# The U buffers of b, f and g moved by 64 bytes, and two pairs of buffers exchanged

## The chip, the cores and the metric

The kernel runs on one core of one Trainium2 chip. A core has five engines with queues of their own: TensorE (PE, matmuls; its weight loads are shown apart as PEld), VectorE (DVE), ScalarE (ACT), GpSimd (POOL) and SyncE (SP, which only issues transfers). They work on SBUF, 128 partitions of on-chip memory; TensorE writes its sums to PSUM, eight banks of 2 KB a partition. The metric is the time of one execution on the device in microseconds (us), as a median of several.

## The reference

One layer of a streaming encoder, on 1024 positions of 1024 channels in float32:

```python
u = rms_norm(x, pre_norm)
z, bg, cg, v = jnp.split(u @ w_in, 4, axis=-1)          # w_in: 1024 x 8192
y = bg * causal_dwconv(cg * v, conv_w) * jax.nn.silu(z)  # three taps, 2048 channels
out = x + rms_norm(y @ w_out, post_norm)                 # w_out: 2048 x 1024
```

Nearly all arithmetic is in the two matrix products, 1024 x 1024 x 8192 and 1024 x 2048 x 1024.

## The kernel before

**Two halves of a number.** A float32 value is split into a high part, rounded to the type that TensorE multiplies (`F32R`, four bytes), and a low part, the rest (`split`: ScalarE copies, VectorE subtracts). One product of two such operands takes three matmuls: low weights by high data, high weights by low data, high weights by high data (`product`, L810). Each of the 4320 matmuls has a weight load of its own, of 128 columns.

**Seven products for eight.** The input product is cut into 2 x 2 blocks, and seven products of sums and differences of blocks, named a to g, take the place of eight. The normed and transposed input, in the seven combinations that the products need, stays in SBUF as seven **U buffers**, u_a to u_g. Each is a tile of 16,384 bytes a partition, `[128, 2, 4, 512]`: a high and a low half, each of four blocks of 128 rows by 512 positions. The weights pass by in 32 *pairs* of column blocks (two pairs, p = 2c and 2c + 1, make one of 16 *chunks*, c), each split into a `wh` and a `wl` tile. So a **wide** product (a, c, d or e of a pair) is twelve matmuls that stream 512 positions of a U buffer past weights that lie in *pages*.

**Once more for b, f and g.** From chunk 2 on, the products b, f and g (f up to chunk 14, g up to chunk 13) are themselves cut in 2 x 2 and done by seven smaller products, a' to g' (`deep_product`, L1404). Such a **narrow** product is six matmuls of 256 positions. Four of the seven, a', b', e' and f', stream a quarter of the U buffer; c', d' and g' stream combinations that lie in tiles of their own, called `ub` (`ubch_deep`, `ufdl_deep` and so on, 2,048 bytes each, in the pool `tmp` behind `gpad`).

**The output product** uses the same scheme. The U buffers are free by then, and their space is taken, buffer by buffer, by the split operands: `ou_` (w_out, the moving operand) and `oy_` (the result y, the weights) for the halves 0 and 1 of a, c, e, d and g (`split_pages`, L1552, and `third_unit`, L1536, for `ou_a1`), and `oA`, `oB` and `ox` for the small products of b and f (`split_small`). Here the moving operand and the weights both lie in U buffers.

**Where things lie.** SBUF is filled in the order of the pools: 1,024 bytes for DMA descriptors, `const`, `small`, `up` (seven buffers of 16,384 bytes from address 3136), `pages` (32 pages of 2,048 bytes from 117824), and then `head` or `tmp` or `p2` in turn from 183360. All addresses here are bytes within a partition. Modulo 128 the U buffers and the pages lie at 64, the ub tiles at 96. The names in the trace are those of the tiles: `px<-u_d,wdh` is a matmul that sums into the PSUM bank px, streams u_d and has weights from wdh; `px2b`, `pv2f` and the like are banks of narrow products, `po_`, `pb_`, `pf_` those of the output product.

**The order of the work.** The program records all operations, and a planner (`Plan.arrange`) puts them in an order for each engine by modelled costs and due times, then emits them (`Plan.emit`, L604). It counts U buffers as one pool of seven and does not know where a buffer lies. Which of the seven an allocation gets is decided on emission: in the kernel before by the pool, in the order in which buffers come free. Because every engine operation passes through one helper, the profile gives the same line, L252, for all of them; so tiles tell them apart.

Of the kernel before, what the change touches and what calls it, by code (L numbers as in the profile page):

```python
# [11 lines left out]
F32 = mybir.dt.float32  # L12
# [77 lines left out]
class View:  # L90
# [3 lines left out]
    def __init__(self, tile, steps, ids, dtype):  # L94
        self.tile, self.steps, self.ids, self.dtype = tile, steps, ids, dtype
# [88 lines left out]
class Pool:  # L184
# [4 lines left out]
    def tile(self, shape, dtype, **kw):  # L189
        t = Tile(self, list(shape), dtype, kw)  # L190
        self.plan.room.setdefault(t.key, kw.get("bufs", self.bufs))
        if not self.plan.recording:
            if kw["tag"] == "pg":
                t.slot = self.plan.slots.pop(0)
            t.get()
            self.plan.taken.setdefault(t.key, []).append(t)
        return t


class Op:  # L200

    __slots__ = ("lock", "order", "base", "move", "others", "lead", "est", "engine", "name", "args", "kw", "n", "needs", "feeds", "dur", "lat", "waits", "late", "tiles", "news", "start", "ideal", "pos", "soft")


class Engine:
# [409 lines left out]
def kernel(  # L615
# [35 lines left out]

    const = plan.pool(ctx.enter_context(tc.tile_pool(name="const", bufs=1)), 1)
    small = plan.pool(ctx.enter_context(tc.tile_pool(name="small", bufs=2)), 2)
    up = plan.pool(ctx.enter_context(tc.tile_pool(name="up", bufs=7)), 7)
    pages = plan.pool(ctx.enter_context(tc.tile_pool(name="pages", bufs=PAGES)), PAGES)
    psum = plan.pool(ctx.enter_context(tc.tile_pool(name="psum", bufs=8, space=bass.MemoryType.PSUM)), 8, "psum")
    dram = plan.pool(ctx.enter_context(tc.tile_pool(name="dram", bufs=1, space=bass.MemoryType.DRAM)), 1, "dram")
# [962 lines left out]
    slots = [("a", 2), ("b", 2)]  # L1620
# [445 lines left out]
```

## Time and profile before

| | us |
|---|---|
| median of 3 runs (772.88 to 773.8) | 773.35 |
| the profiled execution | 772.83 |
| its span, first to last instruction | 771.0 |
| TensorE busy | 762.2 |
| VectorE busy | 673.9 |
| ScalarE busy | 458.8 |
| GpSimd busy | 462.2 |

The granted clock of TensorE was 0.998 of full speed. In the profile "x12" is a count of instructions; a shape such as `128*128 128x256` gives the weights (rows * columns) and the result. The start of a matmul is recorded, its end is modelled, and a matmul's duration overlaps the start of the next. So the time that one takes from the path is the distance between starts.

### The profile page before, as it was taken

Reading aid. Unit: us, or ns where it says so; the run is one execution under the profiler, and the core shown is the slowest. Engines: PE = TensorE matmul, PEld = TensorE weight load, DVE = VectorE, ACT = ScalarE, POOL = GpSimd, SP = SyncE. Lnnn points to the kernel's source line nnn. Section 1 sums busy time; section 2 is a strip of 40 time slices with the busy share of each in tenths; the row PEclk is TensorE's granted clock in tenths of the full one; section 3 lists DMA queues with packets and bytes.
Section 4 is the critical chain, followed back from the end, with each engine's and each line's share of the span. In section 5 each row is a group of like instructions: output and inputs, shape, how many; then the busy total and the mean of one; then the engine's idle time right before and its main releaser. Section 6 shows DMA issues by size and latency. Waiting matters only on the chain.

```text
span 771.0 us, 12816 instructions
## 1 busy us (share of the span) xinstructions
PE 762.2 (99%) x4320; PEld 669.6 (87%) x4320; DVE 673.9 (87%) x1022; ACT 458.8 (60%) x880; POOL 462.2 (60%) x416
## 2 busy tenths in 40 slices
PE   8999999999999999999999999999999999999996
PEld 7888889898889898888888898988888889889885
DVE  6899988989988978989999989798999898877993
ACT  7765678575656565556556565556653656564831
POOL 2519997889575778696789777584739100600321
PEclk9999999999999999999999999999999999999999
DMA  9222325243333547576858474927465998666842
GB/s 318 66 56 82 119 85 152 101 126 131 97 116 96 171 111 209 126 191 158 239 137 254 116 215 107 249 84 213 122 180 174 335 367 293 197 218 206 274 150 109
DMA packets 117137, 130.11 MB, mean 169 GB/s; under 512 B 7320, under 2 KB 74704, under 8 KB 116944
## 3 DMA queue, kind: packets, MB, share of 16 engines
q1 hardware_dynamic: 112560, 120.77, 49.0%
q0 software_dynamic: 4352, 8.39, 7.1%
q8 instruction: 34, 0.56, 0.3%
q14 instruction: 31, 0.25, 0.1%
q10 hardware_dynamic: 160, 0.14, 0.0%
HBM read 101.74 MB, written 44.30 MB: 189 GB/s over the span
## 4 chain that ended last, share of the span: by engine, by line
PE 98%; DVE 1%; DMA 0%; ACT 0%; POOL 0%; issue 0%; POOLq 0%; ACTq 0%
PE px L252 39%; PE pv L252 15%; PE po_x L252 11%; PE px2b L252 5%; PE px2f L252 4%; PE px2g L252 3%; PE po_v L252 3%; PE pp L252 3%; PE pv2b L252 3%; PE pv2f L252 2%; PE pf_x L252 1%; PE pb_x L252 1%; PE py2b L252 1%; PE pv2g L252 1%; PE py L252 1%; PE pf_v L252 1%
## 5 line engine op out<-in xcount | busy, mean ns | idle before, releaser
L252 PE MATMUL px<-u_d,wdh 128*128 128x512 f32 x248 | 76.8, 390 | 0.0
L252 PE MATMUL px<-u_a,wah 128*128 128x512 f32 x248 | 76.7, 390 | 0.0
L252 PE MATMUL pv<-u_e,weh 128*128 128x512 f32 x248 | 76.7, 390 | 0.0
L252 PE MATMUL px<-u_c,wch 128*128 128x512 f32 x248 | 76.6, 390 | 0.0
L252 ACT COPY beside<-raw 128x512 f32<-128x512 f32 x67 | 39.6, 591 | 31.8 <-DVE wal L252 11.0
L252 PEld LDWEIGHTS px<-u_d,wdh 128*128 128x128 f32 x248 | 46.6, 188 | 9.1
L252 PEld LDWEIGHTS px<-u_c,wch 128*128 128x128 f32 x248 | 46.7, 188 | 9.0
L252 PEld LDWEIGHTS px<-u_a,wah 128*128 128x128 f32 x248 | 46.7, 188 | 8.9
L252 PEld LDWEIGHTS pv<-u_e,weh 128*128 128x128 f32 x248 | 46.6, 188 | 8.9
L252 DVE SCALAR_TENSOR_TENSOR cv<-gpad,cw,cv 128x1024 f32<-128x1024 f32 x32 | 49.7, 1554 | 3.4 <-ACT cv L252 3.3
L252 POOL TENSOR_TENSOR sf<-raw,sc 128x512 f32<-128x512 f32 x30 | 44.5, 1482 | 10.9 <-DVE sc L252 6.0
L252 PE MATMUL px<-u_d,wdl 128*128 128x512 f32 x124 | 48.7, 393 | 0.0
L252 PE MATMUL px<-u_a,wal 128*128 128x512 f32 x124 | 48.7, 393 | 0.0
L252 PE MATMUL px<-u_c,wcl 128*128 128x512 f32 x124 | 48.5, 392 | 0.0
L252 PE MATMUL pv<-u_e,wel 128*128 128x512 f32 x124 | 48.5, 391 | 0.0
L252 POOL TENSOR_TENSOR sc<-se,raw 128x512 f32<-128x512 f32 x25 | 36.5, 1460 | 19.0 <-DVE se L252 10.0
L252 ACT COPY sna<-px 128x512 f32<-128x512 f32 x30 | 17.6, 586 | 49.4 <-PE px L252 47.7
L252 POOL TENSOR_TENSOR raw<-raw,raw 128x512 f32<-128x512 f32 x31 | 44.8, 1446 | 3.3 <-DVE se L252 1.9
L252 POOL TENSOR_TENSOR rs_post<-ve_post,minus_half 128x1 f32<-128x1 f32 x7 | 5.4, 784 | 68.1 <-DVE ve_post L252 68.1
L252 POOL TENSOR_TENSOR se<-raw,raw 128x512 f32<-128x512 f32 x22 | 33.1, 1504 | 17.7 <-DMA raw<-in_sc_w_in 5.7
L252 DVE TENSOR_TENSOR wcl<-sc,wch 128x512 fp32r<-128x512 f32 x31 | 31.6, 1020 | 2.6 <-ACT wch L252 2.6
L252 DVE TENSOR_TENSOR sna<-px2b,sna 128x256 f32<-128x256 f32 x56 | 23.2, 413 | 11.9 <-PE px2b L252 11.9
(486 smaller groups left out, 2637.1 us busy)
## 6 DMA issues: line engine op xcount, KB each, us to landing
raw<-in_sc_w_in SPq DMA_DIRECT2D x128, 256.0 KB, 4.6
y_d<-cv SPq DMA_DIRECT2D x16, 512.0 KB, 3.1
s_d<-s SPq DMA_DIRECT2D x32, 256.0 KB, 4.8
t_d<-in_sc_w_out POOLq DMA_DIRECT2D x16, 512.0 KB, 8.2
tb<-in_sc_w_out SPq DMA_DIRECT2D x16, 256.0 KB, 3.0
t_d<-in_sc_w_out SPq DMA_DIRECT2D x16, 256.0 KB, 4.5
t_d<-t_d SPq DMA_DIRECT2D x16, 256.0 KB, 4.5
s<-y_d SPq DMA_DIRECT2D x16, 256.0 KB, 4.7
```

The lines of the kernel that those rows point to most:

```text
L252: getattr(engine, name)(*(self.plain(a) for a in args), **{k: self.plain(a) for k, a in kw.items()})
```

## The change

The pool of seven buffers is replaced by two pools with a gap behind each. Buffers 1, 2, 5 and 6 (those of d, c, a and e) keep their addresses modulo 128. Behind them come 64 unused bytes, then buffers 0, 3 and 4 (of g, f and b), then 448 unused bytes, so that pages and all that follows move by 512 bytes in all. Modulo 128 the U buffers of b, f and g then lie at 0, those of a, c, d and e, and the pages, still at 64, the ub tiles at 96.

A list says which buffer each allocation takes. It is the order that the pool chose before, but for two exchanges in the output stage: `ou_a1` takes buffer 4 and `oy_a1` buffer 6 (before: 6 and 4), and `oy_g0` takes buffer 6 and `ou_g0` buffer 3 (before: 3 and 6).

```diff
+U_LAYOUT = (
+    ((1,2,5,6,), 64),
+    ((0,3,4,), 448),
+)
+U_SLOTS = (5, 4, 2, 6, 1, 3, 0, 0, 5, 2, 4, 6, 1, 3, 0, 5, 2, 6, 4, 1, 6, 3, 0, 2, 4, 5, 6, 1, 0, 3, 2, 4, 5, 6, 0, 4, 1, 5, 6, 3, 2, 0)
+
+def gap(ctx, tc, name, size):
+    if size:
+        ctx.enter_context(tc.tile_pool(name=name, bufs=1)).tile([128, size // 4], F32, tag=name, name=name)
+
+class Shelves:
+    def __init__(self, ctx, tc):
+        self.at, self.slots = {}, list(U_SLOTS)
+        for n, (slots, room) in enumerate(U_LAYOUT):
+            pool = ctx.enter_context(tc.tile_pool(name=f"up{n}", bufs=1))
+            self.at.update({s: pool for s in slots})
+            gap(ctx, tc, f"room{n}", room)
+
+    def tile(self, shape, dtype, tag, **kw):
+        s = self.slots.pop(0)
+        return self.at[s].tile(shape, dtype, tag=f"u{s}", **dict(kw, bufs=1))
...
-    up = plan.pool(ctx.enter_context(tc.tile_pool(name="up", bufs=7)), 7)
+    up = plan.pool(Shelves(ctx, tc), 7)
```

The slots in the order of allocation are: u_a, u_b, u_c, u_e, u_d, u_f, the second half of x (`xb`), u_g; then ou_a0, oy_a0, ou_a1, oy_a1, oB1_b, oB3_b, oA1_b, oA2_b, oB2_b, oA3_b, ox_b, oy_c0, ou_c0, oy_c1, ou_c1, oy_e0, ou_e0, oy_e1, ou_e1, oA1_f, oB1_f, oB2_f, oA2_f, oA3_f, oB3_f, ox_f, ou_d0, oy_d0, oy_d1, ou_d1, oy_g0, ou_g0, oy_g1, ou_g1.

## The prediction

> **What bounds the kernel now.** I read the page first, from the top, for the engine that never rests; then the chain that ended last, inside two short windows, for the length of one product; then the timeline of TensorE, for the distance from one matmul's start to the next.
>
> ```profile
> span 771.0 us, 12816 instructions
> PE 762.2 (99%) x4320; PEld 669.6 (87%) x4320; DVE 673.9 (87%) x1022; ACT 458.8 (60%) x880; POOL 462.2 (60%) x416
> PEclk9999999999999999999999999999999999999999
> PE 98%; DVE 1%; DMA 0%; ACT 0%; POOL 0%; issue 0%; POOLq 0%; ACTq 0%
> ```
>
> TensorE is busy for 762.2 of 771.0 us at full clock, and 98% of the chain lies on it. Other engines are hardly waited for. The change adds and removes no instruction, so beside a wait at the exchanged buffers it can move the time in one way: through the spacing of the 4320 matmuls. A busy share cannot show a spacing, because neighbouring matmuls overlap. The chain, cut into products, can. First a piece before the narrow products begin, then pieces from the middle:
>
> ```profile
> 72.51 2.72 PE pv L252 x12
> ```
> ```profile
> 272.38 2.75 PE px L252 x12
> 275.13 0.70 PE px2b L252 x6
> 275.83 0.70 PE pv L252 x6
> 276.53 0.72 PE px L252 x6
> 277.25 0.72 PE px2g L252 x6
> ```
>
> The twelve-matmul pieces are wide products (512 columns); six-matmul pieces are narrow ones (256 columns). Equal narrow products differ: 0.70 us and 0.72 us. Their operands are seen in the timeline (first column start, second duration):
>
> ```profile
> 275.67 0.28 PE L252 MATMUL pv<-ufgh_deep,dwf 128*128 128x256 f32 x1
> ...
> 276.37 0.28 PE L252 MATMUL px<-u_g,dwg0l 128*128 128x256 f32 x1
> 276.49 0.40 PE L252 MATMUL px<-u_g,dwg0h 128*128 128x256 f32 x2
> 276.73 0.28 PE L252 MATMUL px<-u_g,dwg0l 128*128 128x256 f32 x1
> ...
> 277.81 0.40 PE L252 MATMUL px<-u_a,wal 128*128 128x512 f32 x1
> ...
> 279.20 0.39 PE L252 MATMUL px<-u_a,wal 128*128 128x512 f32 x1
> ...
> 280.56 0.28 PE L252 MATMUL px<-u_g,dwg2l 128*128 128x256 f32 x1
> 280.67 0.28 PE L252 MATMUL px<-u_g,dwg2h 128*128 128x256 f32 x1
> ```
>
> From 275.67 to 276.37 lie six matmuls that stream a ub tile: 0.70 / 6 = 116.7 ns each. From 276.37 to 277.81 lie twelve that stream u_g: 1.44 / 12 = 120.0 ns each. Both groups multiply 256 columns with weights from pages. What differs is the address of the moving operand against that of the weights. Counted through the pools, the U buffers begin at 3136 = 24*128 + 64, and the pages at 117824, also 64 past a multiple of 128. gpad has 4104 bytes, rounded up to a multiple of 32, so the ub tiles behind it begin 96 past one. Relative to the weights the U buffers lie at 0 and the ub tiles at +32 bytes (modulo 128), and +32 is 3.3 ns a matmul faster. The weight loads differ in the same way:
>
> ```profile
> L252 PEld LDWEIGHTS px2b<-ubgh_deep,dwb 128*128 128x128 f32 x56 | 9.5, 188 | 0.5
> L252 PEld LDWEIGHTS py2b<-u_b,dwb0h 128*128 128x128 f32 x56 | 8.7, 192 | 0.0
> ```
>
> A weight load takes 192 ns beside a U stream and 188 ns beside a ub stream. I read the 4 ns as the moving stream and the weight load being in each other's way, more so where both start at the same offset; that is an inference from these rows.
>
> **The change, part by part.** *Shift of b, f and g.* These buffers move to 0 modulo 128; a, c, d, e, the pages (512 bytes further) and the ub tiles (512 further) keep their offset. So U_b, U_f and U_g lie at +64 bytes relative to the weights instead of 0. The narrow products that read them are a', b', e' and f' of each, six matmuls a product, over 14, 13 and 12 chunks: 336 + 312 + 288 = 936 matmuls. The view of windows counts the matmuls on u_b in that stage (third number in brackets):
>
> ```profile
> 105.00:616.00 511.00, 46.90 (x336) 1.00 0.56 159
> ```
>
> All 936 stand on the path, since TensorE never idles there. Their price at +64 is not in the trace. One bound is the 116.7 ns of +32, the nearest row: 936 * 3.3 ns = 3.1 us saved. The lower bound is the shortest narrow spacing there is, 280.56 to 280.67, 0.11 us, the first narrow matmul behind a wide product: 936 * 0.010 us = 9.4 us saved. The bound above is the step of 3.3 ns with the other sign, since nothing excludes that +64 is worse than 0: 3.1 us lost. I take 115 ns, between 116.7 and 0.11 but nearer to the row with many matmuls: 936 * 5.0 ns = 4.7 us saved.
>
> The Trainium skill weighs against this: "SBUF — State Buffer", section "Who interferes with whom", gives TensorE two independent read ports and says that it never waits on anyone. By it the shift is worth 0 and the time stays. The 116.7 ns against 120.0 ns in one engine, at one width and one clock, does not agree with it as it stands.
>
> *Wide products.* A wide product without narrow ones before it takes 2.72 us (226.7 ns a matmul). Behind narrow ones its first six take 1.39 us (277.81 to 279.20) and its last six 1.36 us (279.20 to 280.56): a slow start of 0.03 us. In 14 chunks with eight such products each that is about 112 * 0.03 = 3.4 us. Their own addresses do not change, so I take 0, with bounds from all of it gone (-3.4 us) to twice as much (+3.4 us).
>
> The 228 wide matmuls on U_b, U_f and U_g themselves (48 of the first chunk, 36, 60 and 84 later) I also cost at 0, bounded by the slow start's 5 ns a matmul (0.03 us / 6): 1.1 us either way.
>
> *Output stage.* Moving operands there lie in U buffers, and so do the weights:
>
> ```profile
> 703.26 3.04 PE L252 MATMUL pf_y<-oB_f,oA_f 128*128 128x256 f32 x24
> 706.14 1.12 PE L252 MATMUL pf_x<-oB_f,oA_f 128*128 128x256 f32 x8
> ```
> ```profile
> 742.33 2.88 PE L252 MATMUL po_x<-ou_g,oy_g 128*128 128x512 f32 x12
> ```
>
> Narrow: 706.14 - 703.26 over 24 is 120.0 ns. Wide: (2.88 - 0.39) / 11 is 226 ns, with no slow start. By the list of slots, five narrow products of 24 get the moving operand at +64 (c', g' of b; a', b', f' of f), three the weights at +64 (a', f' of b; c' of f). The net is 48 matmuls at 5 ns, 0.2 us, or nothing; I take 0. Of the ten wide halves, a1, e0, g0 and g1 get the moving operand alone shifted, c1 and d0 both, four none. 192 matmuls at 5 ns bound it at 1.0 us either way; I take 0.
>
> *The two exchanges.* The first pair is ou_a1 and oy_a1: ou_a1 now takes the buffer of U_b, not U_e.
>
> ```profile
> 604.13 0.62 PE L252 MATMUL pv<-u_e,weh 128*128 128x512 f32 x2
> ...
> 605.06 0.40 PE L252 MATMUL pv2b<-u_b,dwb2h 128*128 128x256 f32 x2
> ```
> ```profile
> 605.26 0.62 ACT L252 CAST ou_a<-ru_a 128x512 fp32r<-128x512 f32 x1
> ```
> ```profile
> 624.68 2.66 PE L252 MATMUL po_x<-ou_a,oy_a 128*128 128x512 f32 x11
> ```
>
> U_e is last read until 604.75, U_b until 605.46. The copy that starts at 605.26 must wait 0.2 us more, and ScalarE's queue behind it with it: the other copies of the unit, the product's snaps and VectorE's subtractions. TensorE reads the half a1 only after 624.68, so some 19 us cover it; without them it would be 0.2 us. In the second pair oy_g0 takes the buffer of ox_f and ou_g0 that of oB2_f:
>
> ```profile
> 719.82 0.88 PE L252 MATMUL pf_x<-ox_f,oA_f 128*128 128x256 f32 x6
> ```
> ```profile
> 723.34 0.60 ACT L252 CAST oy_g<-ry_g 128x512 fp32r<-128x512 f32 x1
> ```
>
> ox_f is last read until 720.70, oB2_f before that, and the first copy starts at 723.34, so no wait arises. No DMA is added or moved, on SP's queue or POOL's; the planner sees the same pool of seven and gives the same order.
>
> *The sum.* The profiled execution took 772.83 us, of which 771.0 are the span. 772.83 - 4.7 = 768.1 us for it. The median of the runs, 773.35 us, is 0.5 us higher, so for a median: 773.35 - 4.7 = 768.6 us.
>
> **Rivals.** *The shift does nothing.* If the pattern repeats every 64 bytes, +64 equals 0 and the time stays at 773.3 us. For it speaks that every offset in the trace is a multiple of 32 and only 0 and +32 occur; against it, only that the layout of 128 bytes is as natural. Chance 0.14.
>
> *+64 is worse than 0.* TensorE streams 256 columns while the next 128 weight columns load. If the two streams meet more often when the moving one starts 64 bytes off, the 936 matmuls take 123.3 ns: 773.35 + 3.1 = 776.5 us. It decides as soon as the spacing passes 121.6 ns (1.5 us over 936). For it speaks that wide matmuls behind a change of width need 0.03 us to settle, so a relation between the streams can be bad, and the new kernel alternates between two offsets; against it, that the one other offset in the trace, +32, is better. Chance 0.18.
>
> *The whole overhead goes.* At 0.11 us for all 936 it is 773.35 - 9.4 = 764.0 us, and with the slow starts gone too 760.6. For it speaks that such spacings occur at all; against it, that they occur only once, behind a wide product, and are back to 120 ns one or two matmuls later. Chance 0.12. The Trainium skill, "TensorE: Matmul & The Clock Gate", section "Back-to-back issue gap", gives N / 2.4 + 2.5 ns for the isolated gap, 109.2 ns at 256 columns; an estimate from that page is 936 * 10.8 ns = 10.1 us and 763.2 us. No run so far shows it.
>
> **How the numbers follow.** My forecast, a part of the overhead goes, has 0.56; its own range is 765.2 (the slow starts gone too: 768.6 - 3.4) to 771.4 (116.7 ns, and 1.1 us lost at wide products: 773.35 - 3.1 + 1.1). A difference under 0.2% (1.5 us) cannot be told from none here. Faster: 0.56 + 0.12 = 0.68. Same: 0.14. Slower: 0.18. The range of 8 in 10 takes in the first rival and half of the third, and leaves out the other half (0.06) and most of the second (0.14): 763.5 to 775.0.
>
> **What would show it.** In the profile after, narrow products on u_b, u_f and u_g take 0.69 to 0.70 us instead of 0.72, their weight loads 188 ns instead of 192, and their share of the chain shrinks; products on ub tiles keep 0.70 and wide ones 2.72 to 2.75. The prediction is wrong if u_g's products still take 0.72 us, or if wide products grow beyond 2.75 us by as much as the narrow ones lose, or if TensorE's idle time grows around 605 us.

## The result and the profile after

The changed kernel takes 771.9 us (median of 14 runs, 771.06 to 773.13); the kernel before took 773.8 us in the 14 runs beside it. The ratio is 0.9977, 95% interval 0.9968 to 0.9985. So it is faster, as forecast, by 1.9 us (1.8 us by the ratio), where 4.7 us were forecast. The first rows of the page after, of the part on engines and of the part on the chain:

```profile
span 770.1 us, 12814 instructions
PE 760.5 (99%) x4320; PEld 665.0 (86%) x4320; DVE 677.0 (88%) x1022; ACT 459.4 (60%) x880; POOL 463.0 (60%) x416
PEclk9999999999999999999999999999999999999999
PE 98%; DMA 1%; DVE 0%; ACT 0%; POOL 0%; issue 0%; POOLq 0%; ACTq 0%
```

TensorE is the bound as before, at the same clock. (Line 279 after is line 252 before.) The chain of the kernel after, cut into products; columns are start, length, engine, PSUM bank, line and number of matmuls. The chain counts a piece from the modelled end of the matmul before it, so its times lie 0.16 us behind the starts in the timeline:

```profile
272.68 2.76 PE px L279 x12
...
275.44 0.70 PE px2b L279 x6
276.14 0.70 PE pv L279 x6
276.84 0.68 PE px L279 x6
277.52 0.68 PE px2g L279 x6
...
294.13 0.71 PE px2f L279 x6
```

The two products at 276.84 and 277.52 stream u_g behind products on ub tiles, and take 0.68 us where they took 0.72. The one at 294.13 streams u_f behind a wide product on u_d, and takes 0.71. So at one offset there are two speeds. The timeline of TensorE gives them more sharply (start, duration):

```profile
276.68 0.28 PE L279 MATMUL px<-u_g,dwg0l 128*128 128x256 f32 x1
...
278.04 0.39 PE L279 MATMUL px<-u_a,wal 128*128 128x512 f32 x1
```

Twelve matmuls on u_g lie between the two starts: 1.36 / 12 = 113.3 ns each, where they took 120.0. The product behind a wide one takes 0.71 / 6 = 118.3 ns, and the narrow one that follows it 117.8 ns by the starts. Over the whole timeline 306 of the 936 narrow matmuls on U_b, U_f and U_g now start less than 115 ns before the next, 630 lie at 115 to 121 ns, and the mean is 116.5 ns (before: 119.4, with 53 under 115 ns). The weight loads beside them are down as well (on average over the 936 from 190.8 to 187.8 ns):

```profile
L279 PEld LDWEIGHTS px2b<-ubgh_deep,dwb 128*128 128x128 f32 x56 | 9.5, 188 | 0.5
L279 PEld LDWEIGHTS py2b<-u_b,dwb0h 128*128 128x128 f32 x56 | 8.6, 188 | 0.0
```

**What is given back.** In the first chunk there are only wide products. There the chain of the kernel after reads:

```profile
70.73 2.72 PE px L279 x12
73.45 2.76 PE pv L279 x12
76.22 2.77 PE px L279 x12
78.99 2.76 PE py L279 x12
```

In the chain before, each of these products takes 2.72 us. The product at 73.45 streams u_f, the one at 78.99 u_b: a wide product at +64 takes 2.76 us. The one at 76.22 streams u_a, whose address relative to the weights did not change, and takes 2.77 us: it comes behind a product at another offset. The same in the output stage, where 25 wide matmuls of the half product a1 are cut out of the timeline in each kernel, first the kernel before:

```profile
626.26 5.83 PE L252 MATMUL po_x<-ou_a,oy_a 128*128 128x512 f32 x25
```

and the kernel after:

```profile
626.31 5.89 PE L279 MATMUL po_x<-ou_a,oy_a 128*128 128x512 f32 x25
```

(5.83 - 0.39) / 24 = 226.7 ns a matmul before, (5.89 - 0.39) / 24 = 229.2 ns after.

**The sum.** Each matmul's distance from its start to the next start, added up over the timeline by what it streams, after less before, in us. Distances over 0.3 us, 13 before and 14 to 16 after, nearly all waits or in the first 40 us, are left out, and the groups are scaled to their full number. The last column is the second profile of the changed kernel, from the repeat below:

| what is streamed | forecast | after | again |
|---|---|---|---|
| narrow, U_b, U_f, U_g (936) | -4.7 | -2.70 | -2.70 |
| narrow, ub tiles (702) | 0 | -0.42 | -0.32 |
| wide, U_b, U_f, U_g (228) | 0 | +0.63 | +0.60 |
| wide, U_a, U_c, U_d, U_e (1536) | 0 | +0.85 | +0.75 |
| output stage, wide (480) | 0 | +0.59 | +0.60 |
| output stage, narrow (336) | 0 | -0.78 | -0.77 |
| sum | -4.7 | -1.83 | -1.84 |

In the last column one distance of 0.21 us at 419 us, where a narrow product waits, makes 0.1 us of the difference in the ub row. The sum is what the ratio says, 0.23% of 773.8 us, or 1.8 us. The one profiled execution shows only 771.0 - 770.1 = 0.9 us of it, because two waits fell into it that have nothing to do with spacings. The view of waits has one at the start of the kernel that the execution before does not list:

```profile
PE pk L279 <- DVE ve_pre L279: 0.8, 1, 0.8
```

The first matmul on u_a starts at 12.76 us here and at 12.30 before. In the repeat below it starts at 12.74, so whether the late start belongs to the kernel is open.

The other wait is in the chain near 557 us:

```profile
556.58 2.93 PE px L279 x12
559.51 0.11 issue
559.62 2.98 PE px L279 x12
```

These 24 matmuls took 5.47 us before and take 6.02 us here. The timeline of VectorE has what they wait for:

```profile
555.41 1.23 DVE L279 TENSOR_TENSOR u_g<-ug,u_g 128x512 fp32r<-128x512 f32 x1
...
558.79 0.67 DVE L279 TENSOR_TENSOR wcl<-sc,wch 128x512 fp32r<-128x512 f32 x1
```

The one ends at 556.64 and the other at 559.46, and TensorE's products on u_g and with wcl go on just then. A further run, below, tells whether this wait belongs to the kernel.

In the middle of the program the gain is steady. The same product of two chunks, six chunks apart, before:

```profile
493.90 2.75 PE px L252 x12
```

and after:

```profile
272.68 2.76 PE px L279 x12
...
492.88 2.76 PE px L279 x12
```

A chunk took (493.90 - 272.38) / 6 = 36.92 us and takes (492.88 - 272.68) / 6 = 36.70 us.

### The profile page after: what moved, and what is told of

Its sections match the earlier page's. It is cut to its first block, busy times and chain, and to the rows that moved or that the text cites. A ratio compares the mean times of both kernels' runs of the same rounds, so it can differ in the third digit from the quotient of the medians.

```text
span 770.1 us, 12814 instructions
## 1 busy us (share of the span) xinstructions
PE 760.5 (99%) x4320; PEld 665.0 (86%) x4320; DVE 677.0 (88%) x1022; ACT 459.4 (60%) x880; POOL 463.0 (60%) x416
## 4 chain that ended last, share of the span: by engine, by line
PE 98%; DMA 1%; DVE 0%; ACT 0%; POOL 0%; issue 0%; POOLq 0%; ACTq 0%
PE px L279 39%; PE pv L279 15%; PE po_x L279 11%; PE px2b L279 5%; PE px2f L279 4%; PE px2g L279 3%; PE pp L279 3%; PE po_v L279 3%; PE pv2b L279 3%; PE pv2f L279 2%; PE pf_x L279 1%; PE pb_x L279 1%; PE py2b L279 1%; PE py L279 1%; PE pv2g L279 1%; PE pf_v L279 1%
## 5 line engine op out<-in xcount | busy, mean ns | idle before, releaser
L279 POOL TENSOR_TENSOR sf<-raw,sc 128x512 f32<-128x512 f32 x30 | 46.1, 1537 | 10.3 <-DVE sc L279 5.9
L279 DVE TENSOR_TENSOR wel<-se,weh 128x512 fp32r<-128x512 f32 x31 | 32.1, 1034 | 0.0
```

Source lines behind the costliest of these rows:

```text
L279: getattr(engine, name)(*(self.plain(a) for a in args), **{k: self.plain(a) for k, a in kw.items()})
```

## Experiments

The theory under test is that what counts for the spacing of matmuls is the offset of the moving operand against the weights, so that the shift does it and the exchanges do not matter. Against it stand that the exchanges do something, that the absolute address counts, and that the gain is one of these buffers and not of the offset.

### The two parts of the change alone

The shift without the exchanges:

```diff
-U_SLOTS = (5, 4, 2, 6, 1, 3, 0, 0, 5, 2, 4, 6, 1, 3, 0, ..., 5, 6, 3, 2, 0)
+U_SLOTS = (5, 4, 2, 6, 1, 3, 0, 0, 5, 2, 6, 4, 1, 3, 0, ..., 5, 3, 6, 2, 0)
```

> The shift of 64 bytes alone, without the two exchanges: a1 and g0 of the output stage have their weights, not their moving operand, in a shifted buffer. Theory A (the spacing depends on the offset of the moving operand against the weights modulo 128, so +64 and -64 are the same): a1 and g0 keep the 229 ns a matmul that they have in the changed kernel, the time is 771.9 us within 0.3. Theory B (modulo 256 or more, so +64 and -64 differ): the 96 matmuls of a1 and g0 return to 226.7 ns, 0.2 us less. Rival C (the exchanges bring the gain, the shift nothing): the time is back at 773.8 us and the narrow products on u_b, u_f, u_g at 120.0 ns.

Measured: 772.67 us, ratio 0.9987 (0.9978 to 0.9996). The chunk stages are as in the changed kernel. The output stage is not; the same 25 matmuls of a1, in the timeline of this kernel:

```profile
626.28 5.99 PE L279 MATMUL po_x<-ou_a,oy_a 128*128 128x512 f32 x25
```

(5.99 - 0.39) / 24 = 233.3 ns, against 229.2 ns with the exchanges. Without them a1 and g0 have the weights shifted and not the moving operand: -64 instead of +64. So -64 and +64 are two things, and the pattern does not repeat every 128 bytes. g0 tells the same: 232.5 ns here, 229.2 with the exchanges. By the starts, a1, g0 and g1 take 0.52 us more than in the changed kernel and one narrow product 0.09 us more. The exchanges are worth 0.6 us there; the medians differ by 0.8 us with intervals that overlap.

The exchanges without the shift:

```diff
 U_LAYOUT = (
-    ((1,2,5,6,), 64),
-    ((0,3,4,), 448),
+    ((1,2,5,6,), 0),
+    ((0,3,4,), 512),
 )
```

> Only the two exchanges, with all seven U buffers in one row as before. If the exchanges cost or gain something through their waits, the time moves; the theory of spacings says nothing does, because without the shift every U buffer has the same offset to the weights. Theory: 773.4 to 773.8 us, ratio 1.000, half products a1 and g0 at 226.7 ns a matmul, TensorE not idle around 605 us. Rival (the wait of 0.2 us at the exchanged buffer is seen): 773.6 to 774.0 us, and TensorE's idle time is up around 605 us.

Measured: 773.18 us, ratio 1.0002 (0.9993 to 1.0011), with every spacing of the output stage as in the kernel before. The exchanges cost no wait around 605 us, and gain only together with the shift.

### Relative or absolute

The two groups change places, so that b, f and g keep 64 modulo 256, and a, c, d, e, the pages and the ub tiles lie 64 less:

```diff
-    ((1,2,5,6,), 64),
-    ((0,3,4,), 448),
+    ((0,3,4,), 192),
+    ((1,2,5,6,), 0),
```

> The same differences as in the changed kernel (b, f and g 64 bytes further than a, c, d, e and the weights), but the other absolute addresses: b, f and g stay at 64 modulo 256, while a, c, d, e, pages and ub tiles move to where they lie 64 bytes less far. Theory (what counts is the moving operand's offset against the weights): as the changed kernel, 771.9 us, span 770.1, ratio 0.9977, narrow products on U_b, U_f, U_g at 113.3 ns behind ub products and 117.8 ns behind wide ones, and wide products on them at 229.2 ns. Rival (the absolute address counts): the narrow products stay at 120.0 ns because their operand has not moved, and the time is 773.4 us or is off by some other amount.

Measured: 772.17 us, ratio 0.9984 (0.9975 to 0.9993), span 770.0 us. The chain:

```profile
276.92 0.68 PE px L279 x6
277.60 0.68 PE px2g L279 x6
```

The spacings are those of the changed kernel, in every group of the table above within 0.1 us. Operands that kept their place modulo 256 got the gain, so what counts is a relation and not the absolute address. This run also keeps the distances among the moving operands. That it is the weights against which the offset counts is shown for wide matmuls by the kernel with all seven buffers at +64, below: there all products of the first chunk have one offset, and still take 2.75 us instead of 2.72. For narrow ones the products before count too, as the ub tiles show.

### Other offsets

Only the two gaps between the groups are changed, here for +32; the others are 96 and 416, 192 and 320, 128 and 384:

```diff
-    ((1,2,5,6,), 64),
-    ((0,3,4,), 448),
+    ((1,2,5,6,), 32),
+    ((0,3,4,), 480),
```

> The changed kernel with b, f and g 32 bytes further instead of 64, the offset of the ub tiles. If the offset against the weights is what counts: narrow products on u_b, u_f, u_g at 116.7 ns both behind wide products and behind ub products (936 matmuls, 3.1 us less than before), and their wide products at a spacing that is open, 226.7 to 233 ns (228 matmuls, 0 to 1.4 us more). Time 770.7 to 772.5 us. If a multiple of 64 bytes counts and not the offset as such, 120.0 ns and 773.8 us.

> The changed kernel with b, f and g 96 bytes further. If the relation repeats every 128 bytes and is symmetric, +96 is -32: narrow products at 116.7 ns as at +32. If what counts is how far the moving operand lies ahead of the weights, +96 is past +64: 113.3 ns or less in both places, 936 matmuls, 6.2 us less than before, 767.6 us, less what the wide products lose.

> The changed kernel with b, f and g 192 bytes further: the same as 64 modulo 128, another place modulo 256 (the moving operand lies 64 behind the weights). Theory A (modulo 128): spacing for spacing the changed kernel, 117.8 ns behind wide products, 113.3 ns behind ub products, 229 ns in wide ones, 771.9 us. Theory B (modulo 256): as in the three small output products that have their weights in a shifted buffer, 113.3 ns for all narrow products (936 matmuls by 6.7 ns, 6.2 us less than before), and wide ones at 226.7 ns: 767.6 us.

> U buffers of b, f and g 128 bytes further than the others. The forecast was made on offsets modulo 128; by that +128 is 0 again. Theory A (pattern of 128 bytes): narrow products back at 120.0 ns, wide ones at 226.7 ns, 773.4 us. Theory B (pattern of 256 bytes or more, for which the half products at -64 speak, 233.3 ns against 229.3 ns at +64): some other pair of spacings; every non-zero offset so far has given wide products of 229 to 234 ns, so narrow ones of 117 to 120 ns and wide ones of 229 to 234 ns, 772.5 to 776 us.

Measured, with the mean distance between starts for the matmuls on U_b, U_f and U_g (each ratio is against the kernel before on the same chip):

| offset | narrow, ns | wide, ns | median, us | ratio |
|---|---|---|---|---|
| 0 (before) | 119.4 | 227.3 | 773.8 | 1 |
| +32 | 116.8 | 233.4 | 773.35 | 0.9996 (0.9987 to 1.0006) |
| +64 (after) | 116.5 | 230.1 | 771.9 | 0.9977 (0.9968 to 0.9985) |
| +96 | 119.9 | 234.1 | 777.95 | 1.0057 (1.0044 to 1.0071) |
| +128 | 118.9 | 232.5 | 775.99 | 1.0031 (1.0019 to 1.0043) |
| +192 | 117.7 | 233.2 | 773.96 | 1.0010 (1.0001 to 1.0019) |

A wide product on u_f in the chain of the kernel at +32 (2.72 us before, 2.76 at +64):

```profile
73.59 2.80 PE pv L279 x12
```

No offset but 0 leaves the wide products alone, and +64 takes least of them. That is what makes +64 the best of the six: narrow matmuls gain nearly as much at +32, and the wide ones eat it (1.4 us at the 228, and 1.4 us at the wide matmuls of the output stage). +128 is not 0 again, so the 128 bytes of the forecast are not the period; 256 or more is left, if there is one. +192 would be -64 by a period of 256, and its 233.2 ns agree with a1 at -64 (233.3), but +32 lies as near.

The expectations for single offsets mostly failed. At +32 the time lies above the expected range, because the wide matmuls took the upper end of theirs and the output stage was not counted. At +96 neither 116.7 nor 113.3 ns came, but 119.9. At +192 neither theory held: 117.7 and 233.2 ns. Only +128 came out within its range, that of theory B.

### The ub tiles as a test of the offset

If the offset is what counts, any other narrow operand should show it. The ub tiles lie behind gpad, so a longer gpad moves them: by 32 bytes to +64, in the changed kernel and in the kernel before, and by 192 bytes to +224 in the kernel before (-32 if the pattern repeats every 256 bytes, which no run here shows). The slices that end with gpad get a stated end.

```diff
-    gpad = tmp.tile([P, TAPS - 1 + L], F32, tag="gpad", name="gpad")
+    gpad = tmp.tile([P, TAPS - 1 + L + 8], F32, tag="gpad", name="gpad")
```

> The changed kernel with the 18 ub tiles 32 bytes further: at +64 against the weights instead of +32. 702 narrow matmuls stream them, now at 116.8 ns. Theory (a narrow matmul at +64 takes 113.3 or 117.8 ns, by what it follows): between 702 * -3.5 = -2.5 us and 702 * +1.0 = +0.7 us against the changed kernel, that is 769.4 to 772.6 us; U_g's products behind them keep 113.3 ns only if the offset of the product before does not matter, otherwise they fall back to 117.8 ns (144 matmuls, 0.6 us more). Rival (the gain is that of b, f and g alone, and not of the offset): 771.9 us, ub products still at 116.8 ns.

> The kernel before with only its ub tiles 32 bytes further: +64 against the weights instead of +32, all U buffers at 0. Theory (offset against the weights): 702 matmuls go from 117.4 ns on average to 113.3 or 117.8 ns, that is -2.9 us to +0.3 us, 770.9 to 774.1 us, and no wide product is lengthened, since no wide product streams a ub tile. Rival (the gain is that of the buffers b, f and g, not of the offset): ub products stay as they are and the time is 773.8 us.

> The kernel before with only its ub tiles moved, to -32 against the weights; all U buffers stay at 0 and so all wide products keep their offset. In the changed kernel products on U at +64 run at 113.3 ns behind ub products at +32, and with ub at +64 at 117.8 ns: what went before counts. Theory S (the step of +32 from one product to the next gives the short spacing): U products behind ub products run at 113.3 ns, about 30 matmuls in each of 13 chunks, 390 * 6.7 = -2.6 us, and with no wide product lengthened 770.7 us, under both kernels. Theory L (each offset has its own spacings, and 0 has none under 120 ns): U products stay at 119 to 120 ns, perhaps with a slow start behind ub as in the kernel before, and the time is 773.3 us, 0.5 us more or less by what ub products at -32 take.

Measured: 774.27 us, ratio 1.0015 (1.0006 to 1.0024), in the changed kernel; 774.35 us, 1.0014 (1.0006 to 1.0023), in the kernel before; and 773.41 us, 1.0000 (0.9991 to 1.0009), for +224. The first is 2.4 us above the changed kernel by the medians and 2.9 us by the ratios, outside what was expected; the second is 0.2 us above its range. The chain of the first, at the products that were shown above:

```profile
277.01 0.71 PE pv L279 x6
277.72 0.71 PE px L279 x6
```

The products on ub take 118.1 ns (before 117.4), but the loss is larger at those that follow: u_g's, 113.3 ns in the changed kernel, are back at 117.9 ns, although their own offset is unchanged. So a product's spacing depends on those before it. With ub alone at +64 and U at 0, ub products take 118.2 ns and those on U_b, U_f and U_g 119.5 to 119.9 on average: no gain. And +224 for ub does not give the short spacing to products at 0 behind it (118.6 ns on average). If +224 is -32, the theory falls that the step of +32 from one product to the next is what counts.

### All seven U buffers at +64

```diff
-    ((1,2,5,6,), 64),
-    ((0,3,4,), 448),
+    ((), 64),
+    ((0,1,2,3,4,5,6), 448),
```

> All seven U buffers 64 bytes further than before, a, c, d and e too. Narrow products on U_b, U_f, U_g as in the changed kernel (113.3 ns behind ub products, 117.8 ns behind wide ones). New: the 1536 wide matmuls on U_a, U_c, U_d, U_e go to +64 as well. Theory (a wide matmul at +64 settles at 229.2 ns, at 0 at 226.7 ns): they gain nothing at the start of a product and lose 2.5 ns in the half of a product that has settled, 1536 / 2 * 2.5 = 1.9 us against the changed kernel, 773.8 us; in the output stage moving operand and weights have one offset again, so the half products there are back at 226.7 ns (-0.5 us) and the narrow ones at 120.0 ns (+0.8 us): 774.1 us in sum. Rival (only the change of offset between one wide product and the next costs, not +64 itself): wide products keep 226.7 ns when settled, and the time is 771.9 - 1.2 + 0.3 = 771.0 us.

Measured: 771.08 us, ratio 0.9968 (0.9956 to 0.9980), 3 us better than expected and lower than the changed kernel. The chain, of its second profile:

```profile
73.17 2.75 PE pv L279 x12
...
275.85 0.68 PE px L279 x6
276.53 0.68 PE px2g L279 x6
...
293.06 0.68 PE px2f L279 x6
```

Every wide product takes 2.75 us, in the first chunk too, where it was 2.72. But now the narrow products behind wide ones (293.06) run at 113.3 ns as well; behind the wide product at 0 this one took 118.3. In the two profiles 702 and 714 of the 936 start less than 115 ns before the next, where 306 did. The mean is 114.5 to 114.7 ns, some 4.5 us less than before. This is what the expectation had left out.

### Everything at +64, and ub at +96

If it were only that no product follows one of another offset, putting the ub tiles at +64 as well should bring all narrow products to 113.3 ns: both diffs above together. In the second kernel gpad is 16 elements longer, which puts the ub tiles at +96.

> All seven U buffers and the ub tiles at +64 against the weights, so that no product follows one of another offset. With ub alone at +64 its products took 118 ns, and so did products on U_b, U_f, U_g behind wide ones at 0; with all of U at +64 the narrow products behind wide ones went to 113.3 ns. Theory (what counts is the offset together with that of the product before: at +64 throughout, narrow ones settle at 113.3 ns): 702 ub matmuls from 117.8 to 113.5 ns, -3.0 us, and 936 U matmuls from 114.7 to 113.4 ns, -1.2 us, against the kernel with all of U at +64 (771.1 us); the sum is 766.9 us, and up to 2 us more where VectorE is then the later one (TensorE waited for it by 0.2 to 0.4 us at a time around 408, 418 and 559 us in that kernel): 766.5 to 769 us, below both kernels. Rival (118 ns is what a ub product takes at +64, whatever goes before): ub and what follows it at 118 ns, 702 * 0.2 + 390 * 4 ns = +1.7 us, 772.8 us.

> All seven U buffers at +64, the ub tiles at +96. With ub at +32 the U products behind them settle at 113.3 ns and stay there through the wide products; with ub at +64 everything stays at 118 ns. Theory D (any change of offset before a product at +64 starts the short spacing): U products at 113.3 to 115 ns as with ub at +32, and 120 ns for ub (702 * 3 = 2.1 us), 773.2 us. Theory U (only a step up from +32 to +64 starts it): U products at 118 ns too, 936 * 3.3 = 3.1 us more, 776.3 us.

Measured: 774.33 us, ratio 1.0011 (1.0002 to 1.0020), and 775.15 us, ratio 1.0023 (1.0014 to 1.0032). The chain of the first:

```profile
278.20 0.71 PE px2g L279 x6
...
294.89 0.71 PE px2f L279 x6
```

and of the second:

```profile
278.51 0.71 PE px2g L279 x6
...
295.23 0.71 PE px2f L279 x6
```

The expectation for the first was wrong by 5 us or more: not one of the 936 starts less than 115 ns before the next, and even its rival, 772.8 us, was too low. Of the second, theory U held: the matmuls on U take 117.9 ns on average, those on ub 119.1. The product at 294.89 stands where the one at 293.06 stood above: it streams u_f at +64 behind a wide product at +64, in the same order of work. Its matmuls take 118.0 ns here and 113.3 there. The edit changes only the offset of the ub tiles, which were streamed some products earlier. So at +64 there are two spacings, and each goes on from product to product. A product on a ub tile at +32 can start the short one (not each does: in the changed kernel u_g's product behind a ub product at 282.36 takes 0.71 us), wide products at +64 carry it on, and a wide product at 0 ends it. With ub at +64 or +96 it never starts in these profiles. There is one profile of each, and the executions of the first kernel spread from 772.4 to 776.1 us, so that it never starts in any execution is not shown. So far the runs; what in the hardware keeps up the one or the other spacing, and why +32 starts the short one, is open.

### The repeats

All seven at +64 once more, and the changed kernel once more, on one chip:

> The kernel with all seven U buffers at +64 and the ub tiles at +32 once more, beside the changed kernel on the same chip. Theory (its narrow products on U take 114.7 ns and not 116.5 ns, its wide ones 229 ns, the first chunk loses and VectorE is waited for): 770.5 to 771.5 us, 0.5 to 1.3 us below the changed kernel. Rival (its lower median came from few runs): the same as the changed kernel, 771.9 us.

> The changed kernel once more, for the comparison on one chip and for its waits: 771.9 us, ratio 0.9977. If the waits of TensorE on VectorE around 556 to 560 us belong to the kernel, they stand here too, 0.5 us in sum; if they belong to the one profiled execution, they are gone and the span is about 769.6 us.

Measured: 770.93 us, ratio 0.9969 (0.9957 to 0.9980), and 771.54 us, ratio 0.9981 (0.9972 to 0.9989). The kernel with all seven at +64 is 0.6 us below the changed one on the same chip, but the intervals overlap: likely better than both kernels, and shown only against the kernel before.

The chain of the repeated changed kernel near 557 us:

```profile
556.70 5.49 PE px L279 x24
```

The 24 matmuls that took 6.02 us are back at 5.49: this kernel does not have the wait on VectorE in every execution. The span is 769.7 us, as expected from that. The exchanges alone had such a wait in their profile too, with no loss in the median. In the kernel with all seven at +64 a wait stood there in both profiles, in the second as:

```profile
553.96 1.16 DVE u_g L279
555.12 0.04 issue
555.16 2.80 PE px L279 x11
557.97 0.14 issue
558.10 2.99 PE px L279 x12
```

There VectorE is on the chain, and u_g is not ready when TensorE comes to it. That a faster TensorE brings this on is not shown: the profiles at +128 and with everything at +64, both slower than the kernel before, wait there too (some 0.3 us for wcl and 0.4 us for u_g), and the run with the two groups exchanged does not. The kernel's narrow products on U gain 4.5 us against the kernel before, and the ratio is worth 2.4. In this profile the wide ones' longer spacing takes 0.9 us of the difference, the ub products 0.2 (most of it a wait near 418 us), and the 24 matmuls of these rows start 0.4 us late and take 5.93 us instead of 5.47, 0.9 us in all.

## Why the prediction was right and wrong

**The direction was right, and so was the place.** The 936 narrow products on U_b, U_f and U_g are what got faster, through the offset of the moving operand against the weights, as read from 116.7 against 120.0 ns in the profile before. The run with the two groups exchanged confirms that the offset is relative. The rivals that the shift does nothing and that +64 is worse than 0 fall: the narrow matmuls took 119.4 ns at 0 and 116.5 at +64. The Trainium skill ("SBUF — State Buffer", section "Who interferes with whom") gives TensorE two independent read ports and says that it never waits on anyone. The section is about engines in each other's way; the reading of it by which the shift is worth 0 does not agree with 119.4, 116.5 and 119.9 ns at three offsets.

The weight loads fell from 192 to 188 ns as forecast. But the reason that the prediction read from them, that the two streams are more in each other's way where both start at the same offset, did not hold: wide matmuls are shortest at 0, narrow ones are no better at +96 than at 0, and the loads take 188 to 189 ns at +64 and +96 alike, where the narrow spacing is 116.5 and 119.9 ns. Why the offset counts stays open.

**The first step that failed is the price of +64.** "I take 115 ns" was set between 116.7 and 0.11 us; measured are 116.5 ns on average, from 119.4 and not from the 120.0 of the rows, so 936 of them gave 2.7 us and not 4.7. The lower price makes 1.4 us of the 2.0 us that are missing here, the lower start 0.6. The bound of 0.11 us was misread: in the trace the two starts, 280.557 and 280.671 us, lie 114 ns apart, and two decimals made 110 of it. With 114 the most to be had was 936 * 6.0 = 5.6 us and not 9.4, and the rival that the whole overhead goes had no row for its 764.0 us. By the forecast's own choice, to stay nearer to the 116.7 ns of many matmuls, the price had to be over 115.3 ns. Nor is there one price. A third of the matmuls took 113.3 ns, the rest 117.8 ns. The rows of the profile before do not show what narrow matmuls do at +64, but the wide products' slow start behind narrow ones already showed that a product depends on what went before.

**The second step that failed is the zero for wide products.** The 228 wide matmuls on the shifted buffers lost 0.6 us, within the bound of 1.1 us given for them. The 1536 on the others lost 0.8 us, although "their own addresses do not change": they now follow products of another offset. The bounds of both steps held these values, the zeros did not; together they gave back 1.5 us, where the narrow price left out 2.0. The output stage and the ub products brought 0.6 us that the forecast did not have, so that 2.9 us are missing in sum.

**The output stage came out near zero, by two terms that cancel.** "I take 0" for the narrow products there was -0.8 us, and 0 for the wide halves was +0.6 us. That the sum is near 0 is luck. The ub products were not in the forecast either: they went from 117.4 to 116.8 ns, -0.4 us, most at those that stand behind U products now at +64 (px2g at 281.43 took 0.71 us, at 281.65 it takes 0.70).

**The exchanges cost nothing, for the reason given, but they were not idle.** On ScalarE the forecast wait is there: the copy ou_a starts 0.71 us after the copy that precedes it (604.74 and 604.03 us), where it was 0.48 (605.26 and 604.78). TensorE does not see it at 605 us:

```profile
604.70 0.70 PE px2b L279 x6
605.40 2.77 PE px L279 x12
```

The forecast counted in the output stage how many operands are shifted and not the sign; +64 and -64 differ by 4 ns a wide matmul, and the exchanges turn two half products from -64 to +64.

**What the prediction set as signs against itself** was half there. The products on u_g take 0.68 or 0.71 us, where 0.69 to 0.70 were expected. Wide products did grow beyond 2.75 us, to 2.76 and 2.77, and took back half of what the narrow ones gained (1.5 of 2.7 us). The rival that the whole overhead goes fails. The shortest spacing that held for a product is 113.3 ns; by the Trainium skill ("TensorE: Matmul & The Clock Gate", section "Back-to-back issue gap") the isolated gap would be 109.2 ns at 256 columns and 215.8 at 512, and the shortest that lasted here are 113.3 and 226.7. The measurement decides.

## What to carry to other kernels

Where TensorE is the bound and never idles, look at the distance between starts, not at busy time: products of one width that differ by some per cent are a lead, and a table by what is streamed finds them. Price a change of addresses for every product that streams the moved buffer, wide ones and those behind them included, since a few thousand matmuls at 1 ns are as much as a few hundred at 5. Then try a whole sweep of offsets rather than one, all buffers of a stage together, and look in the profile for the waits on other engines that take part of the gain.

## What the runs showed of the hardware that was not expected

- The offset of the moving operand against the weights changes the spacing, already by 32 bytes, and not with a period of 128: wide matmuls took 226.7 ns at 0, 229.2 at +64, and on average 232.5 to 234.1 at +32, +96, +128 and +192. Narrow and wide ones do not prefer the same offset: narrow ones took 116.5 ns at +64 and 119.4 at 0.
- At one offset, +64, narrow matmuls have two lasting spacings, 113.3 and 117.8 ns. Which one holds was decided by the offset of an operand streamed earlier, and wide products at +64 carried it over.
- The profiled span can miss such a gain: of two profiles of the changed kernel one shows 0.9 us and the other 1.3 us, where the medians show 1.9 and 1.7 us and the sums of the spacings 1.8 us.
